# Spreading per-token scales by transposes of a repeated column, and the conv norm's row sums by one-column products

## The chip, the cores and the metric

The kernel runs on one core of one Trainium2 chip. The core has a matrix engine (TensorE, "PE" in the profile, with its weight loads as "PEld"), a vector engine (VectorE, "DVE"), an activation engine (ScalarE, "ACT"), a general engine (GpSimd, "POOL") and a queue engine (SyncE, "SP") that issues most of the DMA transfers. Each engine takes its instructions in the order in which the program lists them. The metric is the device time of one execution in microseconds; lower is better.

## What is computed

The reference is a trunk of two layers over 512 tokens of 1024 channels. Each layer is a feed-forward block, a mixer and another feed-forward block, all with residuals and all behind an RMSNorm. What matters here is where a number per token (a reciprocal root mean square) multiplies whole rows of channels:

```python
def rms_norm(x, g):
    y = xf * lax.rsqrt(jnp.mean(xf * xf, axis=-1, keepdims=True) + EPS)
    return (y * g.astype(jnp.float32)).astype(x.dtype)

def swiglu(h, w_gate, w_up, w_down):
    return (jax.nn.silu(h @ w_gate) * (h @ w_up)) @ w_down

for l in range(DEPTH):
    x = x + 0.5 * swiglu(rms_norm(x, ffn1_norm[l]), ...)
    h = rms_norm(x, mix_norm[l])
    a, g, q, k, v = jnp.split(h @ w_in[l], splits, axis=-1)
    conv_out = conv_module(a, g, ...)      # GLU, causal conv of 31 taps, rms_norm over 512 channels, silu
    ...
    x = x + jnp.concatenate([conv_out, diff_out], axis=-1) @ w_out[l]
    x = x + 0.5 * swiglu(rms_norm(x, ffn2_norm[l]), ...)
```

## The kernel before

Activations lie with channels on the 128 partitions and the 512 tokens along the free dimension: `x` is eight tiles of 128x512. A norm's scale belongs to a token, that is to a column, and has to be the same on all partitions before it can multiply a tile. The kernel makes it in two steps.

*Row sums* (`rows_rstd`, L217). ScalarE squares each tile (L271), GpSimd adds the squares into one tile `ssum` (L275; in the conv norm `csum`, L655). Four 128x128 transposes on TensorE (L221) put the tokens on the partitions, in a PSUM bank `ps_rows`; VectorE sums each of the four blocks along the free dimension (L225), scales and adds epsilon (L226), and GpSimd raises the 128x4 result to the power -0.5 (`rsqrt`, L214). The result `rs_y` has a token's scale on the token's partition, one column for each block of 128 tokens.

*Spread* (`spread`, L229). VectorE multiplies the identity matrix with each of the four columns, which gives four diagonal matrices side by side, `diag` (128x512, L241). TensorE multiplies a matrix of ones with it (L245): each output partition holds the 512 scales. ScalarE copies the bank into `rb` (L249). With `split=True` the scale is first separated into a high part that is exact in float32r and the rest (L234, L236), and there are two diagonals and two float32r products that add up in the bank; without it there is one float32 product, which the profile shows as two records.

The spread occurs eight times: at the start of each of the four feed-forward blocks (split; L307 and L451), at the start of each mixer (not split; L316) and in each conv norm (not split; L690, in `conv_finish`). At L316 and L451, and in the row sums ahead of them, the products are pinned at a place in TensorE's order (`pin=True`, `keep_in_program_order`). All other instructions are ordered when the program is built, by a scheduler that lists them with its own estimates of their durations; a tile that waits for a free buffer is ordered behind the release.

Products of weights and activations are made as three float32r products of high and low parts (`mm3`, L161: L163, L166, L167). ScalarE makes the high part of a weight chunk (L100) and VectorE, in the mixer's later chunks GpSimd, the low part (L101).

In the first feed-forward block of the first layer the first two column blocks are computed while the inputs still arrive (`lead_products`, L292), and the squares follow the activations' copies on ScalarE. The next block's products are at L450 (row sums pinned ahead of the fifth input tile) and L451 (spread pinned ahead of the fourth). Two pieces of work that belong to the mixers are listed in this block, `make_scalars` (L507: loads the four lambda vectors into a buffer with the tag `diag` (L513), multiplies them on GpSimd (L515), sums on VectorE (L517), exponentials on ScalarE (L519)) and `make_bias` (L487). The tag `diag` has one buffer, the one that the spread's first diagonal uses too.

At the end of the mixer, attention goes on in steps of one query block and one head: scores (L714), exponentials (L718 on VectorE, L722 on ScalarE), combination of two maps (L728), transposes (L735), their copy on ScalarE (L737), products with the values (L744); after four heads a norm and four transposes (L771). `conv_finish` (L689) is listed behind them: row sums of `csum`, the spread, and for each of four channel tiles a product with `rb` on GpSimd (L694), a tanh (L696), a combination on VectorE (L697), a high part (L698) and a low part (L699). Then the output product starts with the four conv tiles (L824 through `mm3`).

## Time and profile before

| | |
|---|---|
| time before, median of 3 runs | 1796.32 us (1795.74 to 1797.79) |
| profiled execution | 1796.31 us |
| span of the profiled execution, first to last instruction | 1794.5 us |
| instructions | 28356 |
| granted TensorE clock | 1.000 |
| TensorE records in L221 / L245 | 32 / 16 |

How to read the lines that follow in the prediction. A timeline row has the start in us, the duration in us (of the whole group where several are merged, as "x4" says), the engine, the source line, the operation, the output tile and after "<-" the inputs, then the shapes; in brackets the engine's idle time before it and what ended it. Matmuls overlap: a record's duration is longer than the distance to the next record, and it is the distance that counts for throughput. A row of a tile's view has minimum, median and maximum duration in ns and the first and last start in us.

### The profile page before, as it was taken

Reading aid. Unit: us, or ns where it says so; the run is one execution under the profiler, and the core shown is the slowest. Engines: PE = TensorE matmul, PEld = TensorE weight load, DVE = VectorE, ACT = ScalarE, POOL = GpSimd, SP = SyncE. Lnnn points to the kernel's source line nnn. Section 1 sums busy time; section 2 is a strip of 40 time slices with the busy share of each in tenths; the row PEclk is TensorE's granted clock in tenths of the full one; section 3 lists DMA queues with packets and bytes.
Section 4 is the critical chain, followed back from the end, with each engine's and each line's share of the span. In section 5 each row is a group of like instructions: output and inputs, shape, how many; then the busy total and the mean of one; then the engine's idle time right before and its main releaser. Section 6 shows DMA issues by size and latency. Waiting matters only on the chain.

```text
span 1794.5 us, 28356 instructions
## 1 busy us (share of the span) xinstructions
PE 1784.6 (99%) x10845; PEld 1590.1 (89%) x10845; DVE 1211.1 (67%) x1863; ACT 896.1 (50%) x1482; POOL 653.6 (36%) x460
## 2 busy tenths in 40 slices
PE   9999999999999999999999999999999999999999
PEld 7899899888788899899888998998887888998997
DVE  6976477568867867477576765765788587673762
ACT  6555265445744456256433643654558354552651
POOL 4242232269843132133102312412797331322420
PEclk9999999999999999999999999999999999999999
DMA  7466476323212366466333654663231133664651
GB/s 243 107 179 183 108 181 176 118 94 94 71 48 83 94 165 188 106 171 189 105 94 98 171 167 120 177 179 118 71 114 51 48 106 91 166 178 112 180 150 59
DMA packets 111721, 231.24 MB, mean 129 GB/s; under 512 B 12151, under 2 KB 33414, under 8 KB 111584
## 3 DMA queue, kind: packets, MB, share of 16 engines
q1 hardware_dynamic: 91488, 191.93, 33.4%
q0 software_dynamic: 19808, 37.33, 12.5%
q8 instruction: 85, 1.39, 0.3%
q14 instruction: 52, 0.43, 0.1%
q10 hardware_dynamic: 288, 0.16, 0.0%
HBM read 227.26 MB, written 3.42 MB: 129 GB/s over the span
## 4 chain that ended last, share of the span: by engine, by line
PE 96%; DVE 2%; issue 1%; ACT 1%; DMA 0%; SPq 0%; ACTq 0%; DVEq 0%
PE ps_pair L384 38%; PE ps_d L166 9%; PE ps_d L163 9%; PE ps_d L167 9%; PE ps_pair L167 5%; PE ps_pair L166 5%; PE ps_pair L163 5%; PE ps_pair L596 2%; PE ps_pair L597 2%; PE ps_pair L598 2%; PE ps_out L163 1%; PE ps_out L166 1%; PE ps_sc L714 1%; PE ps_out L167 1%; DVE actl L263 1%; PE ps_v L628 1%
## 5 line engine op out<-in xcount | busy, mean ns | idle before, releaser
L100 ACT ACTIVATE whi<-wraw 128x1024 fp32r<-128x1024 f32 (+2 forms) x599 | 465.9, 802 | 609.5 <-PE ps_pair L384 225.7
L101 DVE TENSOR_TENSOR wlo<-wraw,whi 128x512 fp32r<-128x512 f32 (+2 forms) x556 | 526.0, 968 | 212.6 <-ACT whi L100 208.4
L384 PE MATMUL ps_pair<-acth,wlo 128*128 128x256 f32 x1088 | 308.5, 284 | 0.0
L384 PE MATMUL ps_pair<-actl,whi 128*128 128x256 f32 x1088 | 308.5, 284 | 0.0
L384 PE MATMUL ps_pair<-acth,whi 128*128 128x256 f32 x1088 | 308.4, 283 | 0.0
L166 PE MATMUL ps_d<-hl,whi 128*128 128x512 f32 x704 | 274.2, 390 | 0.0
L167 PE MATMUL ps_d<-hh,wlo 128*128 128x512 f32 x704 | 273.4, 390 | 0.0
L163 PE MATMUL ps_d<-hh,whi 128*128 128x512 f32 x704 | 268.7, 390 | 0.0
L384 PE MATMUL ps_pair<-th,wlo 128*128 128x256 f32 x816 | 231.3, 283 | 0.0
L384 PE MATMUL ps_pair<-tl,whi 128*128 128x256 f32 x816 | 231.2, 283 | 0.0
L384 PE MATMUL ps_pair<-th,whi 128*128 128x256 f32 x816 | 231.2, 283 | 0.0
L146 POOL TENSOR_TENSOR wraw<-wraw 128x512 f32<-128x512 f32 x68 | 101.8, 1497 | 339.5 <-DMA wraw<-in_gu 272.2
L141 POOL DMA_DIRECT2D wraw<-in_gu x68 | 82.0, 1207 | 392.4 <-DMA wraw<-in_gu 228.6
L384 PEld LDWEIGHTS ps_pair<-acth,whi 128*128 128x128 f32 x1088 | 209.1, 192 | 0.3
L384 PEld LDWEIGHTS ps_pair<-actl,whi 128*128 128x128 f32 x1088 | 209.0, 192 | 0.3
L384 PEld LDWEIGHTS ps_pair<-acth,wlo 128*128 128x128 f32 x1088 | 209.1, 192 | 0.0
L480 DVE SCALAR_TENSOR_TENSOR x<-ps_d,x 128x512 f32<-128x512 f32 x96 | 64.7, 689 | 179.6 <-PE ps_d L167 179.3
L166 PE MATMUL ps_pair<-actl,whi 128*128 128x512 f32 x448 | 175.0, 391 | 0.3
L163 PE MATMUL ps_pair<-acth,whi 128*128 128x512 f32 x448 | 174.4, 394 | 0.5 <-ACT whi L100 0.3
L167 PE MATMUL ps_pair<-acth,wlo 128*128 128x512 f32 x448 | 174.5, 391 | 0.0
L384 PEld LDWEIGHTS ps_pair<-tl,whi 128*128 128x128 f32 x816 | 156.7, 192 | 0.7
L384 PEld LDWEIGHTS ps_pair<-th,whi 128*128 128x128 f32 x816 | 156.7, 192 | 0.6
(176 smaller groups left out, 3268.9 us busy)
## 6 DMA issues: line engine op xcount, KB each, us to landing
wraw<-in_gu SPq DMA_DIRECT2D x208, 256.0 KB, 4.0
wraw<-in_gu SPq DMA_DIRECT2D x104, 512.0 KB, 3.7
wraw<-in_gu POOLq DMA_DIRECT2D x68, 512.0 KB, 5.7
wraw<-in_wqkv SPq DMA_DIRECT2D x24, 512.0 KB, 3.7
wraw<-in_dn SPq DMA_DIRECT2D x84, 128.0 KB, 3.1
wraw<-in_dn SPq DMA_DIRECT2D x32, 256.0 KB, 3.1
wraw<-in_wag SPq DMA_DIRECT2D x16, 512.0 KB, 3.6
wraw<-in_wout SPq DMA_DIRECT2D x16, 512.0 KB, 3.6
```

Source lines behind the costliest of these rows:

```text
L100: S.activation(hi, raw, AF.Copy)
L101: (eng or V).tensor_tensor(out=lo, in0=raw, in1=f32(hi), op=ALU.subtract)
L141: nc.gpsimd.dma_start(two.rearrange("p (b c) -> p b c", b=2), u[:, h[0]].unsqueeze(1).broadcast_to([P, 2, 512]), accum_op=ALU.add)
L146: G.tensor_tensor(more[:, h[0]], two[:, h[1]], whole[:, h[0]], op=ALU.add)
L163: first = T.matmul(ps, wh, xh, start=start, stop=False)
L166: T.matmul(ps, wh, xl, start=False, stop=False)
L167: T.matmul(ps, wl, xh, start=False, stop=stop)
L384: mm = T.matmul(ps, l, r, start=first and i == j == 0, stop=False, skip_group_check=True)
L480: V.scalar_tensor_tensor(x[:, m, :], ps, 0.5, x[:, m, :], op0=ALU.mult, op1=ALU.add)
L596: T.matmul(ps[n], xh[:, t], wh, start=k == 0, stop=False)
L597: T.matmul(ps[n], xh[:, t], wl, start=False, stop=False)
L598: T.matmul(ps[n], xl[:, t], wh, start=False, stop=k == KT - 1)
```

## The change

The spread loses its diagonals. For each of the four columns of `rc` it now takes the column repeated 128 times as the stationary operand of a TensorE transpose against the identity, which puts the same 128 scales on every partition; four such transposes fill the bank. The split into two parts is gone with its two products, and so are the two small VectorE operations that made it; nothing uses the tag `diag` for a diagonal any more. `rows_rstd` stays as it is for the layer norms.

In `conv_finish` the row sums no longer go through `rows_rstd`. Each of the four blocks of `csum` is the stationary operand of a float32 product with one column of ones, which leaves the 128 sums of the block in one column of the bank; the scale and epsilon are applied by one VectorE operation that reads the bank, and the power follows on GpSimd as before. The transposes (L221) and the reduction (L225) are gone there.

```diff
-    def spread(rc, tag, pin=False, split=False):
-
-        parts, dt, left = [rc], F32, ones
-        if split:
-            hi = small.tile([P, NT], F32R, tag="rc_hi", name="rc_hi")
-            V.tensor_scalar(hi, rc, 1.0, None, op0=ALU.mult)
-            lo = small.tile([P, NT], F32, tag="rc_lo", name="rc_lo")
-            V.tensor_tensor(lo, rc, f32(hi), op=ALU.subtract)
-            parts, dt, left = [f32(hi), lo], F32R, ones_r
+    def spread(rc, tag, pin=False):
+
+
         ps = bank("y", "ps_spread")
-        for n, part in enumerate(parts):
-            dg = tmp.tile([P, NT, P], dt, tag=("diag", "sq")[n], name="diag", bufs=1 + n)
-            V.tensor_tensor(
-                dg, ident.unsqueeze(1).broadcast_to([P, NT, P]),
-                part.unsqueeze(2).broadcast_to([P, NT, P]), op=ALU.mult,
-            )
-            mm = T.matmul(ps, left, dg.rearrange("p j c -> p (j c)"), start=n == 0, stop=n == len(parts) - 1)
+        for j in range(NT):
+            mm = T.transpose(ps[:, j * P : (j + 1) * P], rc[:, j : j + 1].broadcast_to([P, P]), ident)
             if pin:
                 tc.keep_in_program_order(mm)
         r = act.tile([P, SEQ], F32, tag=tag, name=tag)
...
-            r = spread(rc, "rb", split=True)
+            r = spread(rc, "rb")
...
-                        r = products(pr, w, held[-1][2][1], 1, 3, lambda: spread(rc, "rb", pin=True, split=True))
+                        r = products(pr, w, held[-1][2][1], 1, 3, lambda: spread(rc, "rb", pin=True))
...
             def conv_finish():
-                rcv = spread(rows_rstd(csum, CC, "c")[0], "rb")
+
+                v = bank("y", "ps_crow")[:, :NT]
+                for j in range(NT):
+                    T.matmul(v[:, j : j + 1], csum[:, j * P : (j + 1) * P], ones[:, :1], start=True, stop=True)
+                vs = small.tile([P, NT], F32, tag="rowvc", name="rowv")
+                V.tensor_scalar(vs, v, 1.0 / CC, EPS, op0=ALU.mult, op1=ALU.add)
+                rcv = spread(rsqrt(vs, NT, "c"), "rb")
                 for c in range(CT):
```

The order that the scheduler makes moves with this. SyncE's order of transfers is unchanged. In the first block the scalars' chain (L513 to L521) is listed from the start of the program: the first load is GpSimd's first DMA; its products stand behind L538, its reduction on VectorE behind the third L101 of 128x128, its exponential on ScalarE ahead of the second L262. The second load stands behind the last L528 on GpSimd, its reduction on VectorE behind three L263 and ahead of the four L101 of 128x512, and its exponential behind the first L100 of 128x512 on ScalarE. The product for the bias (L497) now stands ahead of the first spread. At the end of the mixer the spread's transposes stand earlier among the attention's steps, and the first output product stands later among them.

## The prediction

> **What bounds the kernel now.** I read the page's busy lines first, then the chain of waits, then the busy times by stage, and last the timeline of each engine at the eight places where the scales are spread.

> ```profile
> PE 1784.6 (99%) x10845; PEld 1590.1 (89%) x10845; DVE 1211.1 (67%) x1863; ACT 896.1 (50%) x1482; POOL 653.6 (36%) x460
> PE 96%; DVE 2%; issue 1%; ACT 1%; DMA 0%; SPq 0%; ACTq 0%; DVEq 0%
> 0.00:50.00 50.00, 48.43 (x197) 36.87 (x197) 35.54 (x56) 29.43 (x44) 21.51 (x38) 1.00 0.65 220
> 485.00:512.00 27.00, 24.78 (x151) 19.45 (x150) 26.25 (x92) 22.12 (x66) 11.94 (x13) 1.00 0.00 1
> 512.00:564.00 52.00, 51.86 (x324) 46.37 (x323) 30.39 (x42) 19.37 (x28) 22.32 (x13) 1.00 0.25 72
> ```

> The last three lines give, for a stretch, its length and then the busy us of PE, PEld, DVE, ACT and POOL, the granted clock, and the DMA engines' share and GB/s. TensorE is the bound: 99% of the span, 96% of the chain. So an operation taken off VectorE is worth nothing unless TensorE was waiting for it. There are two places where it does wait: the start (48.43 of 50 us busy) and the end of the mixer, 485 to 512, where VectorE is busy 26.25 of 27 us and TensorE only 24.78. That second stage comes once per layer. A change can also cost time at the start, where three engines feed TensorE just in time.

> **TensorE's own work.** A spread is today one float32 product (two records) at four places, and two float32r products at four others; both become four 128x128 transposes. The trace has four such transposes in L221.

> ```profile
> 31.50 0.60 PE L221 MATMUL ps_rows<-ident,ssum 128*128 128x128 f32 x4
> 31.86 0.48 PE L163 MATMUL ps_pair<-acth,whi 128*128 128x512 f32 x1
> 32.17 0.39 PE L166 MATMUL ps_pair<-actl,whi 128*128 128x512 f32 x1
> ...
> 36.74 0.89 PE L245 MATMUL ps_spread<-diag,ones_r 128*128 128x512 f32 x2
> 37.47 0.39 PE L163 MATMUL ps_pair<-acth,whi 128*128 128x512 f32 x1
> 37.70 0.40 PE L166 MATMUL ps_pair<-actl,whi 128*128 128x512 f32 x1
> ...
> 370.24 1.02 PE L245 MATMUL ps_spread<-diag,ones 128*128 128x512 f32 x2
> 370.69 0.79 PE L163 MATMUL ps_pair<-acth,whi 128*128 128x512 f32 x1
> 371.33 0.40 PE L166 MATMUL ps_pair<-actl,whi 128*128 128x512 f32 x1
> ```

> A 512-column product follows the one before it after 0.23 us (37.47 to 37.70). From the first record of each group to the second product behind it, less 0.23: four transposes 0.67 - 0.23 = 0.44; the float32 spread 1.09 - 0.23 = 0.86; the first split spread 0.96 - 0.23 = 0.73 (part of it a wait for VectorE). The three other split spreads are two products of 0.23, 0.46, against 0.44: nothing. So the two spreads of the mixer's start give 2 x 0.42, the first one 0.29.

> At the conv norm the spread gives 0.42 again, and the row sums take it back: four transposes (0.44) become four float32 one-column products. No row shows a one-column product; the nearest is L744's 128-column one, in the chain of waits.

> ```profile
> 477.82 0.89 PE ps_o L744 x8
> ```

> A float32 product is two records, so four of them are eight: 0.89 from above. From below 0.44, since as many weights must be loaded as now. I take 0.89, because the weight load is the same as L744's: +0.45 per layer. TensorE's sum: -0.84 - 0.29 - 2 x 0.42 + 2 x 0.45 = **-1.1 us** (-2.0 with the lower price).

> **VectorE's removed work outside the conv norm** (two small operations and two of 128x512 at each split spread, one of 128x512 at the mixer's start) lies beside TensorE's products: TensorE doesn't wait for the result there except 0.3 us at the first, already counted. If that cover were gone, about 1.7 us per split spread would count.

> **The end of the mixer.** Here the chain from the squares' sum to the first output product is what TensorE waits for.

> ```profile
> 489.90 0.60 PE L221 MATMUL ps_rows<-ident,csum 128*128 128x128 f32 x4
> 490.54 0.69 DVE L225 TENSOR_REDUCE rowv<-ps_rows 128x4 f32<-128x512 f32 x1
> 492.16 1.01 POOL L214 TENSOR_TENSOR rs_y<-rowv,mhalf 128x4 f32<-128x4 f32 x1 [1.58 <-DVE rowv L226]
> 493.29 0.69 DVE L241 TENSOR_TENSOR diag<-ident,rs_y 128x512 f32<-128x512 f32 x1
> 494.76 1.02 PE L245 MATMUL ps_spread<-diag,ones 128*128 128x512 f32 x2
> 496.34 0.58 ACT L249 ACTIVATE rb<-ps_spread 128x512 f32<-128x512 f32 x1
> 499.62 1.29 DVE L697 SCALAR_TENSOR_TENSOR yp<-th,yp 128x512 f32<-128x512 f32 x1
> 500.95 0.72 ACT L698 ACTIVATE acth<-yp,ghalf 128x512 fp32r<-128x512 f32 x1 [0.59 <-DVE yp L697]
> 501.73 0.51 PE L163 MATMUL ps_out<-acth,whi 128*128 128x512 f32 x1 [1.26 <-ACT acth L698]
> 510.37 0.74 DVE L699 SCALAR_TENSOR_TENSOR actl<-u,ghalf,acth 128x512 fp32r<-128x512 f32 x1
> ```

> Without L225 the row value is ready about 0.5 us earlier, so the power on GpSimd ends near 492.7. In the changed program's order of instructions the spread has moved up on TensorE: one map's values with their wait (1.14), three transposes (0.33) and a score product (0.22) now stand behind it, and the row sums before it are 0.45 longer, so it starts at 494.76 - 1.69 + 0.45 = 493.5. ScalarE's copy stands behind four operations that now end 0.45 later, at 494.8, against 496.34: 1.5 us gained. Through GpSimd's product, the tanh and L697 that grows to 2.0, since fewer operations stand between: L698 at about 498.9 against 500.95.

> But the first output product can't use it. In the changed order it stands behind the values of another attention map, whose copy is queued on ScalarE behind L698, a tanh, a copy and two exponentials (0.62 + 0.61 + 0.27 + 0.45 + 0.39, as they follow one another in this stage): copy at 501.3 to 501.6, values 0.44, product at about 502.1, against 501.73. What is gained is what was done before it and what it no longer waits for after it: VectorE has 1.2 us less to do, and its fourth L699 comes 1.8 us earlier. From 502.1 TensorE has 7.9 us of work (24 products of 0.23, the rest attention) to the point where both conv output banks are full, and I count 1.2 us of waits for the second and third channel: 511.2, with four transposes (0.44) still due that were done by 512.2 before. That is **-0.6 us per layer**, between 0 (TensorE's order eats it all) and -1.8 (TensorE follows VectorE); -1.2 for both. From 512 on TensorE is full (51.86 of 52), so what is gained is kept.

> **The start.** The diagonal tile's buffer was shared with the lambda vectors, and their load waited for the first spread. That tie is gone, and the order puts the scalars' whole chain at the start: two loads on GpSimd's queue, their products, a reduction on VectorE, and an exponential on ScalarE, in the middle of the weights' splitting. ScalarE loses two table loads later, where nothing waits for them.

> ```profile
> 8.80 0.22 POOL L528 TENSOR_SCALAR gq<-gq 128x2 f32<-128x2 f32 x1
> 13.22 2.67 ACT L100 ACTIVATE whi<-wraw 128x512 fp32r<-128x512 f32 x4
> 17.92 0.61 ACT L271 ACTIVATE ssum<-x 128x512 f32<-128x512 f32 x1
> 19.14 11.04 POOL L275 TENSOR_TENSOR ssum<-ssum,sq 128x512 f32<-128x512 f32 x7 [10.12 <-ACT sq L271]
> 26.37 1.06 ACT L100 ACTIVATE whi<-wraw 128x1024 fp32r<-128x1024 f32 x1 [0.51 <-PE ps_pair L166]
> 27.46 1.56 DVE L101 TENSOR_TENSOR wlo<-wraw,whi 128x1024 fp32r<-128x1024 f32 x1 [4.79 <-ACT whi L100]
> 29.08 0.50 PE L167 MATMUL ps_pair<-acth,wlo 128*128 128x512 f32 x1
> ```

> The next rows are the scalars' own (minimum, median and maximum in ns; the load's time from issue to landing in us), and the landings of what SyncE's queue issues between 9 and 17 us.

> ```profile
> L515 POOL TENSOR_TENSOR lamv<-lamv x4: 313/652/2057, 41.1 to 52.9; 128x64 f32<-128x64 f32 x4
> L517 DVE TENSOR_REDUCE lamd<-lamv x2: 278/282/286, 46.7 to 53.2; 128x2 f32<-128x128 f32 x2
> DMA to landing us min/median/max: 3.5/3.5/3.6
> wraw<-in_gu SPq DMA_DIRECT2D x5, 512.0 KB, 7.2
> wraw<-in_gu SPq DMA_DIRECT2D x3, 256.0 KB, 6.0
> ```

> The first exponential costs ScalarE under 2 us near 6 us, where it waited for loads anyway; I price it at nothing (0.5 at most, if the load is late there too). The second load is queued on GpSimd behind L528: 9.02, plus the first pair of products (2 x 0.31, VectorE being idle then) = 9.65. It lands 3.5 us later by its own row, or 6.0 by that of a transfer issued between 9 and 17 us, when the DMA engines are full; I take the middle, 14.4. Products 0.63, reduction 0.33: 15.4. ScalarE stands after its first L100 until then, then has the exponential (0.2) and 4.0 us of copies to the first square, so the squares start 15.4 + 4.3 - 17.9 = 1.8 us late. GpSimd's seven sums move with them, and the next weights' copy at 26.37 is queued behind the squares that wait for those sums. It had 0.5 us to spare (its idle 0.51), VectorE's wlo and TensorE's L167 at 29.08 have none. **+1.3 us** at TensorE, from 0.3 (3.5 us) to 2.5 (6.0 us).

> [...]

> **The sum.** The profiled execution took 1796.31 us with a span of 1794.5, beside a median of 1796.32, so they can stand for each other. 1796.3 - 1.1 - 1.2 + 1.3 = **1795.3 us**.

> **Rivals.**
> 1. The end of the mixer pays in full: TensorE follows VectorE (-1.8 per layer) and the load lands early (+0.3): 1796.3 - 1.1 - 3.6 + 0.3 = 1791.9. For it: 26.25 of 27 us VectorE. Against: the output product's new place.
> 2. The load at the start is late: 7.2 us as the 512 KB row, products at 1.27 the pair (twice the median), so 9.02 + 1.27 + 7.2 + 1.27 + 0.33 = 19.1, the squares 5.5 late, TensorE 5.0; and the mixer gives nothing: 1796.3 - 1.1 + 5.0 = 1800.2. It decides from a landing about 6.9 us after the issue. Against: its own row says 3.5, and it has a quarter to half of those neighbours' bytes.
> 3. The transposes of one repeated column don't overlap: their stationary operand is a column read 128 times, which no row shows. Each then costs its whole 0.27 us (L221 shows four in 0.60), 1.09 instead of 0.44, eight times: 1795.3 + 5.2 = 1800.5. [...]

> **Chances.** A measurement of this kernel tells some 0.2% (3.6 us) from no change. The forecast, no difference of that size, 0.56; rival 1 and its neighbours 0.25; rivals 2 and 3 0.12 and 0.07. The range goes from below rival 1 to just under rivals 2 and 3: 1791.0 to 1800.0; the forecast's own is 1793 to 1798.

> **What would show it.** L221's successor in the spread: four records 0.11 apart (else rival 3). The eight records of the conv row sums: 0.9 us. The rb copy at the conv norm 1.5 us earlier after the row sums than now (6.4 us), and the first output product no earlier. The first square near 19.7 instead of 17.92, and a wait at TensorE near 29 us of a little over a microsecond. If the first square is not late, the start's term is wrong; if the first output product is over a microsecond earlier, the mixer's is. A difference inside the feed-forward blocks after 60 us, where only the order of VectorE's and ScalarE's work changes, would be one that I have not foreseen.

## The result and the profile after

| | median, us | lowest to highest | runs |
|---|---|---|---|
| before | 1796.18 | 1795.74 to 1797.79 | 10 |
| changed | 1801.91 | 1798.54 to 1803.00 | 10 |
| changed, profiled execution | 1798.54 (span 1796.8) | | 1 |

The changed kernel takes 1.0027 times as long, with a 95% interval of 1.0019 to 1.0035: slower, by a quarter of a percent. Two things are to be explained. The profiled execution lies 2.2 us above that of before (1796.31), and the median of the runs lies another 3.4 us higher.

From the page of the changed kernel, busy time by engine and the chain of waits:

```profile
PE 1782.7 (99%) x10869; PEld 1592.1 (89%) x10869; DVE 1210.7 (67%) x1841; ACT 897.4 (50%) x1480; POOL 655.4 (36%) x460
PE 94%; DVE 3%; POOL 1%; ACT 1%; issue 1%; DMA 1%; ACTq 0%; DVEq 0%; POOLq 0%
```

and its busy times in the stretches shown of before, in the same columns (the mixer's end is shifted by the 1.1 us by which it starts later):

```profile
486.10:513.10 27.00, 23.82 (x151) 19.69 (x150) 25.11 (x88) 21.93 (x65) 12.15 (x13) 1.00 0.00 1
513.10:565.10 52.00, 51.88 (x327) 46.65 (x325) 31.61 (x44) 20.07 (x29) 22.35 (x14) 1.00 0.24 72
0.00:50.00 50.00, 46.41 (x192) 35.94 (x193) 33.18 (x52) 27.43 (x45) 21.11 (x40) 1.00 0.67 221
```

TensorE is less busy in both of the stretches where it waited before: 23.82 against 24.78 us at the mixer's end, 46.41 against 48.43 in the first 50 us. VectorE's busy time at the mixer's end did fall, from 26.25 to 25.11 us, so the work was saved, but TensorE got less out of it and not more.

Where the 2.2 us arise is seen best by taking the same product in both traces and subtracting its start before from its start after. I did this for all products that both kernels have:

```
at (us of before)   28     34     42    368    374    480    535   1258   1264   1375   1425   1790
after - before    -0.40  +1.86  +1.53  +1.51  +1.10  +1.12  +1.65  +1.54  +1.13  +1.17  +2.30  +2.23
```

The steps are: +2.3 between 28 and 34 us (the start), -0.3 at the first spread, -0.4 at each mixer's start (368 to 374, 1258 to 1264), +0.5 at the end of the first mixer and +1.1 at the end of the second. Between these places the difference moves by a tenth at most, apart from a dip of 0.2 near 80 us that comes back. The -0.40 with which the row begins is no effect of the change: the kernels below whose start is that of before have 0.0 to -0.6 there.

**The spread** itself does what was forecast. The tile's view (minimum, median and maximum of one in ns):

```profile
L234 PE MATMUL ps_spread<-ident,rs_y x32: 271/272/322, 39.6 to 1465.4; 128*128 128x128 f32 x32
```

Four records of 0.27 us take 0.60 together (the row at 494.65 further down), so they start 0.11 apart, as the transposes of L221 do.

**The start.** The timeline of the changed kernel:

```profile
9.14 0.62 POOL L502 DMA_DIRECT2D lamv<-in_lamv  x1
15.30 0.60 POOL L504 TENSOR_TENSOR lamv<-lamv 128x64 f32<-128x64 f32 x2 [5.53 <-DMA lamv<-in_lamv]
16.31 0.20 ACT L508 ACTIVATE lame<-lamd 128x2 f32<-128x2 f32 x1 [3.04 <-DVE lamd L506]
19.83 0.61 ACT L260 ACTIVATE ssum<-x 128x512 f32<-128x512 f32 x1
21.04 11.04 POOL L264 TENSOR_TENSOR ssum<-ssum,sq 128x512 f32<-128x512 f32 x7 [5.14 <-ACT sq L260]
```

and TensorE's waits in the first 60 us (in total, times, longest):

```profile
PE ps_pair L167 <- DVE wlo L101: 1.5, 1, 1.5
PE ps_pair L163 <- ACT whi L100: 1.1, 2, 0.6
```

The second lambda load lands 6.1 us after its issue, ScalarE stands idle for 3.04 us in front of the exponential that needs it, the squares start at 19.83 instead of 17.92, and GpSimd's sums 1.9 us late. The weights that are split behind those squares reach TensorE late: the 1.5 us and 0.6 of the 1.1 us lie between 28 and 31 us.

**The mixer's end.** The chain from the row sums to the first output product, and the score products L709 that come before it:

```profile
491.02 0.95 PE L682 MATMUL ps_crow<-ones,csum 128*128 128x1 f32 x8
492.77 1.01 POOL L214 TENSOR_TENSOR rs_y<-rowv,mhalf 128x4 f32<-128x4 f32 x1 [1.05 <-DVE rowv L684]
494.65 0.60 PE L234 MATMUL ps_spread<-ident,rs_y 128*128 128x128 f32 x4
495.93 0.60 ACT L238 ACTIVATE rb<-ps_spread 128x512 f32<-128x512 f32 x1
499.08 1.45 DVE L692 SCALAR_TENSOR_TENSOR yp<-th,yp 128x512 f32<-128x512 f32 x1
500.45 0.42 DVE L713 CUSTOM_DVE_ANT_0 ps_sc<-ps_sc,bias 128x256 f32<-128x256 f32 x1
500.56 0.72 ACT L693 ACTIVATE acth<-yp,ghalf 128x512 fp32r<-128x512 f32 x1 [0.33 <-DVE yp L692]
501.19 0.49 PE L709 MATMUL ps_sc<-kt,qz 128*128 128x128 f32 x2 [0.83 <-DVE mn L713]
502.37 0.49 PE L709 MATMUL ps_sc<-kt,qz 128*128 128x128 f32 x2 [0.68 <-DVE e L723]
503.17 0.38 ACT L732 ACTIVATE at<-ps_at 128x256 f32<-128x256 f32 x1 [0.17 <-PE ps_at L730]
504.11 0.50 PE L163 MATMUL ps_out<-acth,whi 128*128 128x512 f32 x1
```

Less the 1.12 us by which this stage starts later, the rb copy is at 494.81 (before 496.34), L693 at 499.44 (its counterpart before, L698, 500.95), but the first output product is at 502.99 (before 501.73). It no longer waits for L693. What TensorE waits for now are two score products in front of it, and these wait for VectorE: L692 of the conv channel, which was early, ran ahead of the attention map's L713.

### The profile page after: what moved, and what is told of

The parts are those of the page before. It is cut to its first block, busy times and chain, and to the rows that moved or that the text cites. A ratio compares the mean times of both kernels' runs of the same rounds, so it can differ in the third digit from the quotient of the medians.

```text
span 1796.8 us, 28378 instructions
## 1 busy us (share of the span) xinstructions
PE 1782.7 (99%) x10869; PEld 1592.1 (89%) x10869; DVE 1210.7 (67%) x1841; ACT 897.4 (50%) x1480; POOL 655.4 (36%) x460
## 4 chain that ended last, share of the span: by engine, by line
PE 94%; DVE 3%; POOL 1%; ACT 1%; issue 1%; DMA 1%; ACTq 0%; DVEq 0%; POOLq 0%
PE ps_pair L373 38%; PE ps_d L167 9%; PE ps_d L163 9%; PE ps_d L166 9%; PE ps_pair L167 5%; PE ps_pair L166 5%; PE ps_pair L163 5%; PE ps_pair L587 2%; PE ps_pair L585 2%; PE ps_pair L586 2%; PE ps_sc L709 1%; PE ps_out L167 1%; PE ps_out L163 1%; PE ps_out L166 1%; DVE actl L252 1%; PE ps_v L615 1%
## 5 line engine op out<-in xcount | busy, mean ns | idle before, releaser
L100 ACT ACTIVATE whi<-wraw 128x1024 fp32r<-128x1024 f32 (+2 forms) x599 | 466.6, 802 | 609.1 <-PE ps_pair L373 224.8
L101 DVE TENSOR_TENSOR wlo<-wraw,whi 128x512 fp32r<-128x512 f32 (+2 forms) x556 | 530.5, 976 | 216.6 <-ACT whi L100 211.3
L166 PE MATMUL ps_d<-hl,whi 128*128 128x512 f32 x704 | 273.9, 389 | 0.0
L167 PE MATMUL ps_d<-hh,wlo 128*128 128x512 f32 x704 | 272.9, 389 | 0.0
L163 PE MATMUL ps_d<-hh,whi 128*128 128x512 f32 x704 | 269.2, 389 | 0.0
L167 PE MATMUL ps_pair<-acth,wlo 128*128 128x512 f32 x448 | 174.3, 391 | 1.5 <-DVE wlo L101 1.5
L166 PE MATMUL ps_pair<-actl,whi 128*128 128x512 f32 x448 | 174.8, 391 | 0.3 <-DVE actl L252 0.2
L163 PE MATMUL ps_pair<-acth,whi 128*128 128x512 f32 x448 | 173.7, 392 | 1.1 <-ACT whi L100 1.1
## 6 DMA issues: line engine op xcount, KB each, us to landing
wraw<-in_gu SPq DMA_DIRECT2D x208, 256.0 KB, 4.5
wraw<-in_gu SPq DMA_DIRECT2D x104, 512.0 KB, 3.7
wraw<-in_gu POOLq DMA_DIRECT2D x68, 512.0 KB, 5.7
wraw<-in_wqkv SPq DMA_DIRECT2D x24, 512.0 KB, 3.7
wraw<-in_dn SPq DMA_DIRECT2D x32, 256.0 KB, 3.3
wraw<-in_wag SPq DMA_DIRECT2D x16, 512.0 KB, 3.7
wraw<-in_wout SPq DMA_DIRECT2D x16, 512.0 KB, 3.6
```

Of the source, the lines that this page charges most:

```text
L100: S.activation(hi, raw, AF.Copy)
L101: (eng or V).tensor_tensor(out=lo, in0=raw, in1=f32(hi), op=ALU.subtract)
L163: first = T.matmul(ps, wh, xh, start=start, stop=False)
L166: T.matmul(ps, wh, xl, start=False, stop=False)
L167: T.matmul(ps, wl, xh, start=False, stop=stop)
```

## The clock between the runs

The result lists, for each run, the mean clock that TensorE was granted. In the profiled execution it is 1.000; over the ten runs:

```
mean clock   1.000          0.999          0.998          0.997
runs         2              2              4              2
us           1798.5-1799.4  1800.5-1800.8  1801.7-1802.6  1802.5-1803.0
```

The time goes with the clock; the two runs with a full clock average 1799.0, so the lost clock is some 2.9 us of the median. A mean lower by 0.001 is what half a clock for 3.6 us makes (2 x 0.001 x 1797). The experiments below therefore look at two things: which place costs time at a full clock, and which place costs clock.

## Experiments

One table for all, medians in us, each with the runs of before that were made beside it (1796.1 to 1796.2); "below 1" counts the runs with a mean clock of 0.999 or less.

| kernel | median (lowest to highest) | ratio, 95% interval | below 1 |
|---|---|---|---|
| early_scalars | 1798.99 (1798.44 to 1800.53) | 1.0016, 1.0008 to 1.0025 | 5 of 11 |
| late_scalars | 1799.62 (1798.31 to 1802.34) | 1.0021, 1.0012 to 1.0030 | 5 of 11 |
| crow_only | 1795.60 (1795.03 to 1799.63) | 0.9998, 0.9989 to 1.0007 | 1 of 11 |
| spread_only | 1797.71 (1796.76 to 1798.20) | 1.0008, 1.0000 to 1.0017 | 0 of 11 |
| after_again | 1800.22 | one run | 1 of 1 |
| hold_rb | 1801.59 (1800.33 to 1803.12) | 1.0031, 1.0019 to 1.0044 | 4 of 6 |
| hold_spread | 1798.87 (1797.87 to 1800.83) | 1.0014, 1.0005 to 1.0023 | 2 of 11 |
| best_mix | 1799.33 (1797.28 to 1800.86) | 1.0014, 1.0006 to 1.0023 | 6 of 11 |
| keep_first | 1798.14 (1796.47 to 1800.39) | 1.0011, 1.0002 to 1.0020 | 6 of 11 |
| kf_spread | 1795.50 (1794.63 to 1799.21) | 0.9995, 0.9987 to 1.0004 | 0 of 11 |
| kf_best | 1794.70 (1794.35 to 1795.02) | 0.9991, 0.9982 to 1.0000 | 0 of 11 |
| kf_fill | 1801.00 (1800.73 to 1801.98) | 1.0027, 1.0017 to 1.0037 | 0 of 8 |

Of the 85 runs of the kernel before made beside these, one was below 1 (1799.49 us). Two more lie high at a full clock (1798.45 and 1798.87), so now and then 2 us are lost in some other way, in the kernel before too.

### early_scalars: the start alone

```
-            t = tmp.tile([P, SEQ], F32, tag="diag", name="lamv", bufs=1)
+            t = tmp.tile([P, 4 * HD], F32, tag="lamv", name="lamv", bufs=1)
...
-            pr = t[:, 4 * HD : 6 * HD].rearrange("p (n d) -> p n d", n=2)
+            pr = lv[:, ::2, :]
```

> The kernel before with one thing of the change: the lambda scalars' chain at the start (their tile has a tag of its own, and the products are written over the loaded vectors). Theory A, the start's late chain costs time itself and its wait also costs granted clock: TensorE's wait near 29 to 31 us grows by about 1.7 us, so 1797.9 with a full clock, and most runs lie above that, 1799 to 1802, at a mean clock of 0.997 to 0.999. Theory B, the clock is lost at the mixer's end: the same 1.7 us, every run within 1797.5 to 1798.5 and the clock 1.000 in all. Theory C, the clock differs by chip and not by kernel: the runs of the kernel before on this chip spread as widely.

The six runs with a full clock are at 1798.4 to 1799.0, 2.3 to 2.9 us above before; the five others at 1799.6 to 1800.5. So the scalars' chain at the start costs time by itself, a little more than expected, and clock as well. Theory C falls: the runs of before beside it all kept their clock. The profile is of a run that lost some; its stretch view has the length, then busy us of PE, PEld, DVE, ACT and POOL, the granted clock, and the DMA share and GB/s:

```profile
4.66:8.07 3.41, 1.57 (x7) 0.88 (x6) 1.76 (x6) 1.00 (x4) 2.56 (x9) 1.00 0.93 285
8.07:11.49 3.42, 3.42 (x10) 2.64 (x9) 2.70 (x7) 3.08 (x7) 2.28 (x6) 0.50 0.91 294
11.49:14.90 3.41, 3.41 (x16) 2.79 (x15) 2.45 (x4) 2.00 (x3) 0.00 (x0) 1.00 1.01 312
```

The clock is exactly half for 3.41 us, directly behind 3.41 us in which TensorE was busy for 1.57. The wait in that stretch is not the exponential's:

```profile
6.88 0.86 ACT L100 ACTIVATE whi<-wraw 128x128 fp32r<-128x128 f32 x3 [2.04 <-DMA wraw<-in_gu]
17.66 0.20 ACT L519 ACTIVATE lame<-lamd 128x2 f32<-128x2 f32 x1 [3.27 <-DVE lamd L517]
```

TensorE's first weights came late. Their 64 KB transfers landed after 5.0 us here, after 3.0 in before and after 3.9 and 3.4 in the two profiles of the changed kernel, so the first lambda load, which now runs beside them, probably delays them; that was not tested by itself. The exponential at 17.66 delays the squares as in the changed kernel, but costs less: TensorE's step at 28 to 34 us is +1.1 here.

### late_scalars, hold_rb: the scalars held back elsewhere

late_scalars gives the lambda vectors rb's buffer; hold_rb lets one GpSimd copy from the first rb (`spreads` collects the rb tiles) write into their tile before the load.

```
-            t = tmp.tile([P, SEQ], F32, tag="diag", name="lamv", bufs=1)
+            t = act.tile([P, SEQ], F32, tag="rb", name="lamv")
```

```
+            if l == 0:
+                G.tensor_scalar(t[:, :1], spreads[0][:, :1], 1.0, None, op0=ALU.mult)
```

> The changed kernel with the scalars' chain held back until the first rb has been read (lamv takes rb's buffer). Theory A: the start is as before, clock 1.000 in every run; what is left is the spreads' gain (-0.2 -0.4 -0.4) and the two mixers' loss (+0.5 and +1.1, as the trace of the changed kernel has them): about 1796.8, with runs as close together as those of the kernel before. Theory B: 1797 to 1801 with clocks of 0.997 to 1.000. Theory C: as the kernel before on this chip.

> The changed kernel with the scalars' chain held behind the first spread by one small copy from rb, so that it runs where the kernel before has it (late_scalars held it back to 73 us, where it cost 3 us by itself). With the start's cost gone and the rest as in the changed kernel's trace: -0.2 -0.4 -0.4 for the spreads, +0.5 and +1.1 for the mixers: 1796.8 in runs with a full clock, up to 1.7 more for each mixer whose waits are followed by 3.41 us at half clock; some runs at a mean clock of 0.999 and 0.998, none at 0.997. If the mixer's waits cost no clock, all runs are within 1796.3 to 1797.5.

Both came out some 3 to 5 us above the forecast. The same-product difference says why: in late_scalars it is -0.7 at 60 us and +3.0 at 104, in hold_rb -0.9 and +3.3. The chain had only been moved to a place where it hurts in another way. In hold_rb ScalarE stands 7.77 us in front of the late exponential, and a hidden product of the first feed-forward block waits:

```profile
61.45 0.20 ACT L513 ACTIVATE lame<-lamd 128x2 f32<-128x2 f32 x1 [7.77 <-DVE lamd L511]
...
66.94 0.73 PE L163 MATMUL ps_d<-hh,whi 128*128 128x512 f32 x2 [1.94 <-ACT hh L415]
```

As a test of the start these two are lost. For the clock they are not. The stretch view of late_scalars, whose start is not busy with the chain, has its half clock at the end of the first mixer:

```profile
501.62:505.03 3.41, 1.88 (x13) 1.31 (x11) 3.41 (x12) 2.90 (x10) 2.81 (x3) 1.00 0.02 5
505.03:508.44 3.41, 3.34 (x11) 2.85 (x12) 2.99 (x12) 2.08 (x7) 0.91 (x1) 0.50 0.00 0
```

So theory B holds as well as A: the start and the mixers both cost clock.

### crow_only and spread_only: one half of the change each

```
-                rcv = spread(rows_rstd(csum, CC, "c")[0], "rb")
+                v = bank("y", "ps_crow")[:, :NT]
+                for j in range(NT):
+                    T.matmul(v[:, j : j + 1], csum[:, j * P : (j + 1) * P], ones[:, :1], start=True, stop=True)
...
+                rcv = spread(rsqrt(vs, NT, "c"), "rb")
```

crow_only is this edit on the kernel before; spread_only is late_scalars with this edit undone.

> The kernel before with the conv norm's row sums by one-column products, all spreads as before. By my prediction's step: TensorE's work +0.45 per layer; the row value about 0.5 us earlier. If the mixers' loss comes from the row sums' own length, +0.9 in all: 1797.1. If it comes from where the order puts the first output product, this order has it behind fewer attention products than the changed kernel's, so 1796.0 to 1797.0. Clock 1.000 under theories A and B alike, unless B's wait at the mixer's end is in this order too.

> The changed kernel without the one-column row sums (the conv norm's row sums by transposes and a reduction, as before), and with the scalars held back as in late_scalars: the spreads by transposes alone. By the trace of the changed kernel the spreads outside the conv norm give -0.2 -0.4 -0.4, those at the conv norm -0.4 each, if the mixer's order takes nothing back: 1794.4; if it takes back as much as in the changed kernel, 1796.5. Clock 1.000 under theory A.

crow_only came out below both of its expectations. By the same-product difference it gains 0.3 and 0.2 us at the two mixers' ends. The rest of its gain is at the start, where nothing was changed and where profiles differ by some tenths. spread_only came out above both, because it has the late chain's cost (+2.9 at 104 us); then it has -0.4 at each mixer's start and -0.1 and 0.0 at the mixers' ends. So neither half costs anything at the mixer's end; the loss of 0.5 and 1.1 us exists only with both.

### after_again: the changed kernel, a second profile

> The changed kernel unchanged, for a profile that has the clock drop in it: eight of its ten runs had a mean clock below 1. Theory A+B, a stretch of 3.41 us at half clock follows a stretch in which TensorE waited a good part: the profile has one to three such stretches, each directly behind the waits near 5 to 9, 28 to 31, 496 to 504 or 1387 to 1395 us, none inside a feed-forward block, and the time is 1798.9 plus 1.2 to 1.7 us for each. Theory C, the clock falls at places that have nothing to do with waits: it lies somewhere in a block where TensorE is full.

One stretch at half clock, behind the waits of the second mixer:

```profile
1392.06:1395.47 3.41, 1.84 (x11) 1.46 (x12) 3.41 (x15) 3.02 (x9) 2.81 (x3) 1.00 0.00 0
1395.47:1398.89 3.42, 3.42 (x13) 2.93 (x13) 2.85 (x10) 1.87 (x6) 0.63 (x1) 0.50 0.00 0
```

The first profile of the changed kernel has its least busy stretch there too, but cut elsewhere, and so has before. Neither is followed by a lower clock:

```profile
499.94:503.36 3.42, 1.91 (x14) 1.49 (x13) 3.42 (x11) 2.92 (x10) 2.82 (x4) 1.00 0.02 5
```

```profile
499.81:503.22 3.41, 2.07 (x14) 1.52 (x13) 3.41 (x11) 2.82 (x12) 3.33 (x4) 1.00 0.02 5
```

The half-clock stretches begin a whole number of 3.413 us after the first clock record of their profile (in the rows of early_scalars above, 4.66 to 14.90, three stretches make 10.24 us), and that record's place against the program differs from run to run (4.1 to 6.9 us after the first instruction). The page's busy time is not quite the measure: hold_rb has a stretch of 1.58 us busy, at 63.4, that kept its clock. Counting each product instead by the pace at which its kind follows itself in the trace (0.23 us for 512 columns, 0.11 for a record of 128, 0.22 for a float32 record of 256), and dividing by 3.413, the stretch before a drop is filled to 0.329 in early_scalars, 0.334 in keep_first (below), 0.339 in late_scalars and 0.348 in after_again. Up to TensorE's last products, the least filled ones without a drop have 0.38 (keep_first, second mixer), 0.39 (late_scalars, second mixer, and the changed kernel's first profile) and 0.41 (hold_rb); the one at 63.4 us has 0.42. These figures place a product at the start of its record. Placed at the record's end the same four are still the least filled, but the gap is gone (0.393 against 0.397), so these profiles place the limit only roughly. Slid over all places up to TensorE's last products, such a stretch never falls under 0.395 in the profile of before, but to 0.32 in either mixer of the changed kernel, and to 0.24 near 28 us. So by these figures it depends on where the stretches happen to be cut whether the changed kernel loses clock, and before, as profiled, is out of reach of it there wherever they are cut. Behind its last products before has a stretch at half clock too, which costs no product:

```profile
1790.05:1793.46 3.41, 0.81 (x4) 0.35 (x2) 0.69 (x1) 0.00 (x0) 0.00 (x0) 1.00 0.20 77
1793.46:1794.50 1.04, 0.00 (x0) 0.00 (x0) 0.00 (x0) 0.00 (x0) 0.00 (x0) 0.50 0.00 0
```

One of the 85 runs of before and one of the eleven of crow_only lost a stretch all the same; no profile shows where. The count of lost stretches can be checked too. If the grid lies anywhere with equal chance and the limit is 0.36 (an estimate, between the 0.348 and the 0.38 above), each profile gives the lost stretches per run that are to be expected: 0.4 for early_scalars and 0.5 for late_scalars and keep_first, where the runs' mean clocks show 0.45, 0.45 and 0.55; but 0.8 for the changed kernel (0.9 by its second profile) and for hold_rb, where they show 1.6 and 1.3. So half of what the changed kernel loses is not accounted for by its profile.

### hold_spread, best_mix: two halves on hold_rb

hold_spread is hold_rb with the conv norm's row sums as before; best_mix is hold_rb with the conv norm's spread as before.

> As hold_rb, with the conv norm's row sums as before (transposes and a reduction): the spreads by transposes alone. spread_only had the same order in the mixer and lost nothing there (-0.1 each). So 1796.2 -0.2 -0.4 -0.4 -0.2 = 1795.0, and a full clock in nearly all runs. If the mixer's loss belongs to the spread, 1796.5 and clocks below 1.

> As hold_rb, with the conv norm's spread by the diagonal tile and a product as before: transposes at the six other spreads, one-column row sums kept. Its order in the mixer is that of crow_only, which gained 0.3 us per mixer by its trace. So 1796.2 -0.2 -0.4 -0.4 -0.6 = 1794.6, with a full clock in nearly all runs. If the mixer's loss comes from the row sums alone, 1796.5 or more.

Both carry hold_rb's cost before 104 us (+2.7 and +3.5 there), so their times miss the expectation by about that. At the mixers' ends the differences move by -0.1 and 0.0 (hold_spread) and by -0.3 each (best_mix), as expected. Their runs below a full clock (2 and 6 of 11) are not explained. The new wait near 64 us is a candidate, and in hold_rb a stretch slid over it falls to 0.35; but in these two profiles it stays at 0.55 and 0.44.

### keep_first, kf_spread, kf_best: start as before

The diagonal tile is kept for the first spread alone, which ties the scalars to where they were:

```
-  r = products(pr, w, held[-1][2][1], 1, 3, lambda: spread(rc, "rb", pin=True))
+  r = products(pr, w, held[-1][2][1], 1, 3, lambda: spread_diag(rc, "rb", pin=True, split=True))
```

spread_diag is the old spread. kf_spread has the old row sums besides; kf_best keeps the new row sums and uses spread_diag for the conv norm's spread too, so that five of the eight spreads are transposes.

> The changed kernel, except that the first spread alone is still made with the diagonal tiles: that ties the lambda scalars to where the kernel before has them, and GpSimd's order at the start is the same as before. This separates the start from the mixers without the 2 to 3 us that every other place of the scalars cost between 60 and 104 us. Expected: no difference up to 360 us, then -0.4 +0.5 -0.4 +1.1 from the trace of the changed kernel: 1797.0 with a full clock. By the trace of the changed kernel TensorE's least busy 3.41 us in each mixer has 0.32 of matmul streaming, and the three profiles with a drop had it right behind a stretch of 0.33 to 0.35: so a part of the runs, 2 to 6 of 11, at a mean clock of 0.999 or 0.998 and 1.0 to 1.7 us later for each; median 1797.5 to 1799. If the clock is only lost at the start, all runs are within 0.8 us of 1797.0.

> As keep_first, with the conv norm's row sums as before (transposes and a reduction): transposes for seven spreads, nothing else. Its mixer order is that of spread_only, whose mixers lost 0.1 us less than nothing each and whose least busy 3.41 us has 0.48. Expected 1796.2 -0.8 -0.2 = 1795.2 with a full clock in every run.

> As keep_first, with the conv norm's spread still by the diagonal tile: one-column row sums and transposes at the six other spreads. Its mixer order is that of crow_only (-0.3 us per mixer, least busy stretch 0.45). Expected 1796.2 -0.8 -0.6 = 1794.8 with a full clock in every run: the fastest of all.

All three came out as expected (kf_spread 0.3 above, with one run at 1799.21 and a full clock, unexplained like the two of before). keep_first's five runs at a full clock average 1797.25, the six others 1799.15, and its profile has the drop at the first mixer:

```profile
498.36:501.78 3.42, 1.82 (x13) 1.33 (x11) 3.42 (x12) 2.88 (x9) 2.82 (x3) 1.00 0.02 5
501.78:505.19 3.41, 3.41 (x13) 2.92 (x13) 2.98 (x11) 2.00 (x6) 0.77 (x1) 0.50 0.00 0
```

What separates it from kf_best is one spread, made by transposes or by the diagonal tile. TensorE's waits between 488 and 514 us (in total, times, longest), of the changed kernel and then of kf_best:

```profile
PE ps_sc L709 <- DVE e L723: 1.0, 2, 0.7
PE ps_sc L709 <- DVE mn L713: 0.8, 1, 0.8
PE ps_out L163 <- ACT acth L693: 0.6, 1, 0.6
PE ps_at L730 <- ACT at L732: 0.4, 1, 0.4
```

```profile
PE ps_out L163 <- ACT acth L716: 0.8, 1, 0.8
PE ps_at L753 <- ACT at L755: 0.4, 1, 0.4
```

Before, the first output product waited 1.3 us and two transposes and products behind ScalarE's copies 0.4 and 0.2. With kf_best's order that wait shrinks to 0.8 and no score product waits.

### kf_fill: work put into the waits

```
                 pt = bank("tp", "ps_at")
+                if i < 2:
+                    T.matmul(pt[:, :256], ones, csum[:, :256], start=True, stop=True)
```

The edit stands on keep_first. The product is overwritten by the map's transposes.

> As keep_first, with one product of 256 columns into the bank of each of the eight last attention maps of a layer, overwritten by the map's transposes: work that is not needed, put where TensorE waits. If low streaming in a stretch of 3.41 us is what takes the clock, the mean clock is 1.000 in all runs, though the waits' causes are as in keep_first; the time is between 1797.0 (the products fit into the waits) and 1803.9 (16 x 0.43 us on top). If the clock has another cause, the runs' clocks fall as often as in keep_first.

All eight runs kept a mean clock of 1.000, where 6 of 11 of keep_first lost some; the least filled stretch slid over the mixers is 0.44 instead of 0.32. It costs more than it saves (4.0 us above the 1797.0 of a full clock, of 16 x 0.43 = 6.9 us put in). But it shows that what took the clock here was how little TensorE streamed in such a stretch, and not what it waited for: in the first mixer of its profile TensorE still waits 2.2 us, 1.5 of them in front of score products for VectorE.

## Why the prediction was wrong, step by step

- **TensorE's own work: right.** The mixers' starts gave -0.41 each (forecast -0.42), the first spread -0.33 (-0.29), the other split spreads -0.07 at most (0). The eight one-column records took 0.95 us (0.9). Rival 3, transposes that don't overlap, fell: 0.11 apart.
- **VectorE's removed work elsewhere: right.** Nothing moved inside the feed-forward blocks.
- **The start: mechanism right, size too small.** The first square was forecast near 19.7 and came at 19.83, and the wait sits where it was put. The load took 6.1 us, just past the end of the range I had given, where I took the middle (its products then at 15.30, not 14.4), and TensorE's step at 28 to 34 us is +2.3 against +1.3. With the first spread's gain the start's steps come to +1.9, a microsecond more than the forecast's 1.3 - 0.3; half of that is hidden in the pair of profiles by the -0.40 with which they begin. Rival 2 had its time near the measured one, but not its mechanism: the load never took 6.9 us.
- **The end of the mixer: wrong in sign.** I forecast -0.6 per layer and had +0.5 and +1.1. The chain was right up to the copy (4.91 us after the row sums, 4.9 forecast), and L693 half a microsecond late (499.44 for 498.9). The step that failed is the one after: "copy at 501.3 to 501.6, values 0.44, product at about 502.1". It priced the attention map in front of the output product by ScalarE's queue alone, and counted TensorE's waits only behind that product. The copy came at 502.05 (503.17 less 1.12) and the product at 502.99, because two score products that TensorE's order puts ahead of that map's transposes wait for VectorE, which is full here (0.83 and 0.68 us in the rows above). These 0.9 us are most of the 1.1 between forecast and result in the first mixer. In all there are 1.0 + 0.8 + 0.6 + 0.4 = 2.8 us of waits (the four rows of the changed kernel above) against 1.3 + 0.4 + 0.2 = 1.9 before. What was early in the conv chain came at the cost of an attention map. crow_only and kf_spread show that neither half does it alone; the order of the whole does. Why the second mixer loses twice as much as the first was not tried; it is not a matter of the second mixer alone, since in the changed kernel's second profile the first mixer lost 1.0 us at a full clock.
- **The clock: no term at all.** All stretches that I read had a granted clock of 1.00 and I took it as fixed. This is about half of the miss, and what put the median outside the range: 2.9 to 3.4 us of the 6.6. Waits at the start (early_scalars) and in the mixers (late_scalars, keep_first, after_again) left one stretch of 3.41 us filled to 0.329 to 0.348, and the next 3.41 us ran at half clock. These figures count the transposes as products like any other: with them the four stretches before a drop are the four least filled of all fourteen profiles up to TensorE's last products; without them before has one of 0.275 that kept its clock and early_scalars one of 0.329 that lost it.

The sum at a full clock, 1796.3 + 1.5 - 0.8 + 0.5 + 1.1 - 0.1 = 1798.5, is the profiled execution, and it lies within the range given. The median lies 1.9 us above the range. How the lost clock divides between the start and the two mixers in the median run stays open, as does the half of it that the profile does not account for. A drop was seen at 8 us (early_scalars), in the first mixer (late_scalars, keep_first) and in the second (after_again), none in a profile behind the wait near 30 us, and the runs list only their mean.

## What to carry to other kernels

A buffer that two unrelated tiles share is also an order: before removing a tile, see what else is allocated under its tag, and where that work goes when the tie is gone. Where a stage is bound by a full engine and an order made for the whole stage, a piece that gets faster moves other pieces behind it; count the waits in front of the point you watch as well as behind it. The version to keep here is kf_best: the one-column row sums, and transposes at all spreads but the first and the conv norm's. Its gain is small, 1.5 us with an interval that touches no change, though all eleven of its runs (1794.4 to 1795.0) lie below all of before's beside it (1795.6 and up).
